# A SwiGLU layer by seven-product blocks: gate and up one product at a time in doubled banks, and the down projection with other signs, bank order and visits

## The chip, the core and the metric

The kernel is one inference step of a decoder layer and runs on one NeuronCore of a Trainium2 chip. It drives TensorE (PE, matrix products; PEld is its weight load), VectorE (DVE), ScalarE (ACT), GpSimd (POOL) and SyncE (SP, which here issues most DMAs). [...] The metric is the device time of one execution in microseconds (us), as the median of several runs.

## What is computed

The layer is attention and a gated delta rule on one projection, cross attention, and then SwiGLU. Only the last part changes:

```python
# x: 512 prompt rows and 32 sample rows of 2048 features; hidden width 5632
h = rmsnorm(x) * norm_ffn_g
gate, up = split(h @ w_gate_up)      # 2048 -> 2 x 5632
y = x + (silu(gate) * up) @ w_down   # 5632 -> 2048
```

All of it is held to float32 accuracy. A float32 matrix is therefore split into a high part (rounded to the float32r form that PE multiplies) and a low part (the rest), and a product is three: high by high, high by low, low by high.

## The kernel before

All 544 rows (T) are the columns of the moving operand; HT = 272 is half of them. Gate/up and down are both computed in 2 by 2 blocks with seven products instead of eight (the Winograd form of Strassen's scheme): two blocks of weight rows by two blocks of weight columns against two feature blocks by the two halves of T. The weight side needs four sums of weight blocks, the moving side four sums of feature blocks, and each result is a combination of the seven products. A matmul is 128 by 128 by 272.

**Gate/up** (lines 1740 to 1763 and the loop in `go`). There are 44 output blocks of 128 gate and 128 up columns. A block is four steps, a step takes two pairs of feature blocks and issues 7 products × 2 pairs × 3 terms = 42 matmuls (L1678). A step's products go to four accumulators: P16 (products 1 and 6, two banks), P7 (one), P45 (two), P23 (two), seven banks in all, held once. In the first three steps all high terms come first and then the low terms; in the last the terms go product by product. After the last step `combine` reads the banks (L1706 on ACT, L1707 to L1713 on DVE), then DVE scales by the row norm (L1731, L1732), ACT applies silu (L1726) and DVE multiplies (L1735).

**Weights of a step** (`Left`): SP loads two 256 KB pieces (raw, L1627) four steps ahead; POOL makes two sums of 256 columns (L1635, L1636) and DVE the two that depend on them (L1640, L1641); ACT rounds 768 raw and 1024 summed columns to high parts (wh, L1646); DVE subtracts them for the low parts (wl, L1653).

**Hidden values.** For each pair of finished blocks POOL makes the four moving-side sums (L1573 to L1576), ACT rounds (L1858), POOL makes low parts (L1859), and SP stores seven tiles to DRAM (hT, L1861).

**Down.** Sixteen output columns of 128, in eight blocks of two, against eleven groups of hidden pairs. Only a few groups fit in SBUF, so a block is visited several times (VISITS): each visit accumulates one or two groups, one step of 42 matmuls each. At the end of a visit the banks are taken to SBUF: first and seeded ones by an ACT copy (L1772), P16 and P7 by a DVE addition (L1770). At the start of a later visit P45 and P23 are seeded from SBUF by an ACT copy (L1759), in the last visit all four banks. POOL issues the loads of a group's 14 tiles (pr, L1835). After its second visit a block gets the residual x: SP loads two tiles (xl, L1780) into two slots, and POOL adds them (L1784 to L1786). The last visits are of groups 9 and 10 for all eight blocks, sixteen steps in a row; then the results are combined, transposed through PE (L961), scaled by ACT (L1968) and stored.

**What sets the order.** The FFN is written in a fixed order by `go`: for each step each engine's instructions stand in the order in which the code emits them, and no scheduler moves them. Each engine works through its own queue in that order, so an instruction that waits holds up what stands behind it on the same engine, DMA issues of SP and POOL among them.

## Time and profile before

| what | us |
|---|---|
| median of 3 runs | 3054.19 (3053.77 to 3056.27) |
| the profiled execution, its own time | 3052.51 |
| its span, first to last instruction | 3050.7 |
| first to last matmul of gate/up and down (L1678) | 1510.0 to 3037.1 |
| PE / DVE / ACT / POOL busy in the span | 2890.4 / 2265.9 / 1455.2 / 1149.7 |

The profile is of one execution. A group of instructions is named by its line, engine and operation, and by the tiles that it writes and reads (out<-in); behind the bar stand its busy time, the mean length of one in ns, and the idle time of its engine just before it with what ended that idle time. Matmuls are pipelined: each row lasts 0.29 us, but the next starts sooner, so PE can be busy all the time at different speeds. DMA issues are counted as they are issued; when a transfer lands is a separate entry.

### The profile page before, as it was taken

The numbers are of one execution on the slowest core, as the hardware profiler recorded it, in microseconds if no ns is written. First come the engines' busy times: TensorE is split into PE (matmuls) and PEld (weight loads), VectorE is DVE, ScalarE is ACT, GpSimd is POOL, SyncE is SP. The second block draws the span as 40 slices with busy tenths as digits, with TensorE's granted clock in tenths as the row PEclk, the third lists the DMA queues.
The fourth block names the chain that finished last, engine by engine and source line by source line (L and its number), as shares of the span: only waits on it lengthen the run. The fifth ranks groups of instructions, "written<-read, shape, count | busy, mean of one in ns | idle before, by whom it ended". The sixth has DMA issues, their size and how long they took to land. (4 is left out here: it accounts for less than half of the span.)

```text
span 3050.7 us, 58945 instructions
## 1 busy us (share of the span) xinstructions
PE 2890.4 (95%) x22118; PEld 2773.2 (91%) x22118; DVE 2265.9 (74%) x3513; ACT 1455.2 (48%) x2760; POOL 1149.7 (38%) x1444
## 2 busy tenths in 40 slices
...
GB/s 213 96 80 84 75 89 96 147 134 147 173 105 152 222 205 149 125 86 113 180 88 138 149 138 133 143 148 137 139 141 146 134 222 216 218 190 174 173 143 73
DMA packets 638647, 435.62 MB, mean 143 GB/s; under 512 B 38715, under 2 KB 568968, under 8 KB 638360
## 3 DMA queue, kind: packets, MB, share of 16 engines
...
## 5 line engine op out<-in xcount | busy, mean ns | idle before, releaser
L1678 PE MATMUL bank<-pr,wh 128*128 128x272 f32 x7392 | 1149.7, 291 | 70.1 <-ACT bank L1759 31.1
L1678 PEld LDWEIGHTS bank<-pr,wh 128*128 128x128 f32 x7392 | 1031.2, 190 | 89.9 <-ACT bank L1759 40.6
L1678 PE MATMUL bank<-pr,wl 128*128 128x272 f32 x3696 | 703.9, 289 | 1.2 <-DVE wl L1653 1.2
L1678 PEld LDWEIGHTS bank<-pr,wl 128*128 128x128 f32 x3696 | 556.9, 188 | 5.6 <-DVE wl L1653 5.6
L209 PE MATMUL mm<-ah,wh 128*128 128x272 f32 (+1 forms) x2464 | 538.1, 298 | 4.6 <-ACT ah L322 3.5
L209 PE MATMUL mm<-al,wh 128*128 128x272 f32 (+1 forms) x2464 | 524.2, 291 | 0.7 <-DVE al L240 0.7
L209 PE MATMUL mm<-ah,wl 128*128 128x272 f32 (+1 forms) x2464 | 515.6, 290 | 0.1
L1653 DVE TENSOR_TENSOR wl<-sum,wh 128x1024 fp32r<-128x1024 f32 x264 | 431.2, 1633 | 31.4 <-ACT wh L1646 30.6
L1646 ACT CAST wh<-sum 128x1024 fp32r<-128x1024 f32 x264 | 277.0, 1049 | 326.6 <-DVE sum L1641 322.2
L1635 POOL TENSOR_TENSOR sum<-raw 128x256 f32<-128x256 f32 x264 | 219.3, 831 | 561.3 <-DVE wl L1653 549.8
L1646 ACT CAST wh<-raw 128x768 fp32r<-128x768 f32 x264 | 220.6, 836 | 414.8 <-PE bank L1678 309.1
L209 PEld LDWEIGHTS mm<-ah,wh 128*128 128x128 f32 (+1 forms) x2464 | 391.6, 188 | 27.6 <-issue 8.5
L198 DVE TENSOR_TENSOR wl<-wr,wh 128x512 fp32r<-128x512 f32 (+1 forms) x366 | 262.7, 721 | 192.9 <-ACT wh L197 183.6
L209 PEld LDWEIGHTS mm<-al,wh 128*128 128x128 f32 (+1 forms) x2464 | 389.5, 188 | 5.4 <-issue 2.0
L209 PEld LDWEIGHTS mm<-ah,wl 128*128 128x128 f32 (+1 forms) x2464 | 386.4, 188 | 2.5 <-DVE wl L198 0.5
L197 ACT CAST wh<-wr 128x512 fp32r<-128x512 f32 (+1 forms) x366 | 224.3, 615 | 328.6 <-PE mm L209 272.2
L1653 DVE TENSOR_TENSOR wl<-raw,wh 128x768 fp32r<-128x768 f32 x264 | 293.3, 1111 | 86.0 <-PE bank L1678 75.6
L1636 POOL TENSOR_TENSOR sum<-raw 128x256 f32<-128x256 f32 x264 | 249.4, 945 | 0.0
L1641 DVE TENSOR_TENSOR sum<-raw,sum 128x256 f32<-128x256 f32 x264 | 199.3, 755 | 9.0
L1640 DVE TENSOR_TENSOR sum<-sum,raw 128x256 f32<-128x256 f32 x264 | 163.2, 618 | 7.2 <-POOL sum L1635 7.2
L1859 POOL TENSOR_TENSOR hs<-x,hs 128x544 fp32r<-128x544 f32 x44 | 76.1, 1729 | 52.8 <-issue 42.3
L1859 POOL TENSOR_TENSOR hs<-u,hs 128x272 fp32r<-128x272 f32 (+1 forms) x44 | 79.1, 1797 | 43.9 <-ACT hs L1858 43.9
...
## 6 DMA issues: line engine op xcount, KB each, us to landing
...
hT<-hs SPq DMA_DIRECT2D x154, 272.0 KB
pr<-hT POOLq DMA_DIRECT2D x154, 272.0 KB, 3.7
page<-in_cache_sb_k SPq DMA_DIRECT2D x128, 128.0 KB
...
```

The lines of the kernel that those rows point to most:

```text
L197: nc.scalar.copy(hi[:, :m, :n], raw[:, k : k + m, :n])
L198: nc.vector.tensor_sub(lo[:, :m, :n], raw[:, k : k + m, :n], hi[:, :m, :n].bitcast(F32))
L209: c.nc.tensor.matmul(ps[:n, h, :HT], l[:, :n], r[:, h * HT : (h + 1) * HT], start=first and i == 0, stop=last and i == 2,)
L1635: g.tensor_sub(self.sum[:, 2], a[:, 0], a[:, 2])
L1636: g.tensor_add(self.sum[:, 0], a[:, 0], a[:, 1])
L1640: v.tensor_add(b[:, 1], b[:, 2], a[:, 1])
L1641: v.tensor_sub(b[:, 3], a[:, 3], b[:, 1])
L1646: self.c.nc.scalar.copy(hi, x())
L1653: self.c.nc.vector.tensor_sub(lo, x, hi[:, :, :].bitcast(F32))
L1678: self.c.nc.tensor.matmul(self.c.bank[bank][:, o], self.left.part(low, li, i), r, start=new and not (i or low or n), stop=self.last and i ...
L1859: self.later(0, "pool", lambda: c.nc.gpsimd.tensor_sub(lo[:, o : o + n * HT], x[i][:, : n * HT], hi[:, : n * HT].bitcast(F32)))
```

## The change

**Gate/up.** A block is no longer four steps of two pairs but seven products, one after the other, in the order 1, 5, 6, 2, 7, 3, 4, each over all eight pairs: 24 matmuls into one bank. There are banks A, B and C, two sets used by blocks in turn, and one bank E for both. The combination happens in the banks: after product 1, ACT copies A to B (so that product 2 is added to it), after product 6 A to C (product 3 is added), and product 5 goes from E to SBUF (e). DVE then needs one operation on 272 columns for each quarter, and the row norm is applied to gate only where it is read; up's factor is left out there and made good where y is stored (`unscale`; and the residual x is multiplied by q, the inverse of both norms' factors).

Weights of a block are four loads of 512 KB (L1702), four sums of 1024 columns, all on DVE (L1708), seven high parts on ACT (L1715) and seven low parts on DVE (L1719), made two products ahead. All weight tiles share 13 slots of 4 KB. Of the eight pairs of x the last two are made while the first products run (ticks −1, 0, 2 and 3, a tick being one product), and four extra matmuls (`open`) touch the banks that ACT writes first.

**Down.** All three remaining sums are on DVE (L1757 to L1759: 512, 256 and 256 columns). The signs of the moving-side sums change with them. Visits that are not a block's last use the order 4, 5, 2, 3, 1, 6, 7, last visits 1, 6, 7, 4, 5, 2, 3. The visits are cut in another way: each block's first visit is of one group (for the second half of the blocks the second visit too), and at the end stand four blocks with groups 9 and 10 and four with 10 alone, twelve steps. The first two groups' operands are fetched from four and six ticks before the end of gate/up. The residual needs one tile slot for q, so x comes through one slot; POOL multiplies (L1851) and adds (L1853, L1854, L1856).

**The order.** `Work.at(tick, place, do)` notes what is emitted at which place of a tick; in gate/up a tick is a product, in down a step.

The diff, cut to its core:

```diff
-VISITS = ((0, (0,)), (1, (0, 1)), (0, (1, 2)), (1, (2, 3)), (0, (3, 4)), (1, (4, 5)), (0, (5, 6)), (1, (6, 7)), (0, (7, 8)), (1, (8,)),
-          (0, (9, 10)), (1, (9, 10)))
+VISITS = ((0, (0,)), (1, (0,)), (1, (1,)), (0, (1, 2)), (1, (2, 3)), (0, (3, 4)), (1, (4, 5)), (0, (5, 6)), (1, (6, 7)), (0, (7, 8)), (1, (8, 9)))
+LAST = (9, 10), (10,)
...
+W_TILES = 13
...
+    def at(self, tick, place, do):
+        self.n += 1
+        self.todo.setdefault(tick, []).append((place, self.n, do))
...
+GU_ORDER = (1, 5, 6, 2, 7, 3, 4)
...
+        for x, tick in (("21", -8), ("11", -8), ("22", -7), ("12", -3)):
+            at(self.t0 + tick, 5, lambda x=x: self.load(x))
+        for q, tick in ((7, -4), (5, -3), (6, -2), (3, 1)):
+            at(self.t0 + tick, 50, lambda q=q: self.sum(q))
+        for i, q in enumerate(GU_ORDER):
+            at(self.t0 + i - 2, 20, lambda q=q: self.high(q))
+            at(self.t0 + i - 2, 60, lambda q=q: self.low(q))
+            at(self.t0 + i, 30, lambda q=q: self.matmuls(q))
+        A, B, C, E = f.gu_banks[j % 2]
+        s, v = f.c.nc.scalar, f.c.nc.vector
+        g, u = [], []
+        rr = f.t_rr if j == 0 else 0
+        def left():
+            g.append(f.c.tt("g"))
+            v.tensor_mul(g[0][:, :HT], B, f.rr[:, :HT])
+        def lower():
+            u.append(f.c.tt("u"))
+            v.tensor_add(u[0][:, HT:], A, self.e)
+        def right():
+            v.tensor_add(g[0][:, HT:], C, self.e)
+            v.tensor_mul(g[0][:, HT:], g[0][:, HT:], f.rr[:, HT:])
+        def gate():
+            v.tensor_mul(u[0][:, :HT], A, g[0][:, :HT])
+            v.tensor_mul(u[0][:, HT:], u[0][:, HT:], g[0][:, HT:])
+            f.hidden(j, u[0])
+        def keep():
+            self.e = f.c.tt("e")[:, :HT]
+            s.copy(self.e, E)
+        at(self.t0 + 1, 10, lambda: s.copy(B, A))
+        at(self.t0 + 2, 10, keep)
+        at(self.t0 + 3, 10, lambda: s.copy(C, A))
+        at(max(rr, self.t0 + 4), 40, left)
+        at(self.t0 + 5, 40, lower)
+        at(max(rr, self.t0 + 6), 41, right)
+        at(max(rr, self.t0 + 6), 65, lambda: s.activation(g[0], g[0], AF.Silu))
+        at(max(rr, self.t0 + 6) + 1, 16 if j == NH - 1 else 42, gate)
...
+    def sum(self, q):
+        x, y = {5: ("21", "22"), 7: ("21", "11"), 6: ("22", 7), 3: ("12", 6)}[q]
+        self.a[q] = self.f.tile(F32, "sum")
+        self.f.c.nc.vector.tensor_sub(self.a[q], self.a[x], self.a[y])
...
+        bank = {5: E, 2: B, 3: C}.get(q, A)
+        terms = [(self.hi[q], i, r) for i in range(8) for r in range(2)] + [(self.lo[q], i, 0) for i in range(8)]
+        for n, (w, i, r) in enumerate(terms):
+            self.f.c.nc.tensor.matmul(
+                bank, w[:, i * P : (i + 1) * P], self.f.pairs[i].op[q][r], start=q in (1, 5) and n == 0, stop=n == 23, skip_group_check=True,
...
+    def sums(self):
+        a, v = self.raw, self.c.nc.vector
+        self.sum = b = self.f.tile(F32, "sum").rearrange("p (s m) -> p s m", s=4)
+        v.tensor_sub(b.rearrange("p (x s) m -> p x s m", s=2)[:, :, 0], bc(a[:, 0:1], [P, 2, 2 * P]), a[:, 1:3])
+        v.tensor_sub(b[:, 1], a[:, 1], b[:, 2])
+        v.tensor_sub(b[:, 3], a[:, 3], b[:, 1])
...
-        self.last = self.visit == 5
-        self.seeds = (P16, P7, P45, P23) if self.last else (P45, P23)
+        self.order = (1, 6, 7, 4, 5, 2, 3) if self.visit == self.end else (4, 5, 2, 3, 1, 6, 7)
+        self.seeds = () if not self.visit else (P45, P23, P16, P7) if self.visit == self.end else (P45, P23)
...
+        if bank in (P16, P7) and not new:
+            self.c.nc.vector.tensor_add(x, x, self.c.bank[bank])
+        else:
+            self.c.nc.scalar.copy(x, self.c.bank[bank])
...
-        y, z = (self.c.cst.tile([P, T], F32, tag="rstd", name="xl", bufs=2) for _ in range(2))
-        for i, x in enumerate((y, z)):
-            self.f.later(1, "sp", lambda i=i, x=x: self.c.nc.sync.dma_start(x, self.c.xT[self.m + i]))
-        def add():
-            g = self.c.nc.gpsimd
-            g.tensor_add(self.z, self.z, z)
-            g.tensor_add(self.y, self.y, y)
-            g.tensor_sub(self.y[:, HT:], self.y[:, HT:], z[:, HT:])
-        self.f.later(2, "pool", add)
...
+    def residual(self, tick):
+        c, at = self.c, self.f.work.at
+        xs = {}
+        def load(i):
+            xs[i] = c.cst.tile([P, T], F32, tag="rstd", name="xl", bufs=2)
+            c.nc.sync.dma_start(xs[i], c.xT[self.m + i])
+        def add(i):
+            g, x = c.nc.gpsimd, halves(xs[i])
+            y, z = self.parts[P23], self.parts[P45]
+            g.tensor_mul(x, x, halves(self.f.q))
+            if i:
+                g.tensor_add(z, z, x)
+                g.tensor_sub(y[:, 1], y[:, 1], x[:, 1])
+            else:
+                g.tensor_add(y, y, x)
+        for n, i in enumerate((1, 0)):
+            at(tick + 1 + n, 3, lambda i=i: load(i))
+            at(tick + 2 + n, 2, lambda i=i: add(i))
...
+        tiles = [(pair, n, k) for n in (3, 1, 2, 0) for pair in range(2) for k in range(2 if n else 1)]
+        for g in range(11):
+            a, b = used[g - 3][1] + 1 if g > 2 else (0, 1, 5)[g], used[g][0] - 1
+            for i, x in enumerate(tiles):
+                tick = t0 + a + i * min(b - a, 7) // 14 if g else t0 - (6 if i < 6 else 4)
+                at(tick, 90, lambda g=g, i=i, x=x: self.fetch(g, i, *x))
...
+        early = lambda n: tick - n if p >= n else self.t_down - 2 * (n - p)
+        at(early(4) if p >= 4 else self.t_down - 12 + 2 * p, 95, s.load)
+        at(early(2), 45, s.sums)
+        for i in range(2):
+            at(early(1), 20 + i, lambda i=i: s.high(i))
+            at(early(1), 50 + i, lambda i=i: s.low(i))
+        if p == 0:
+            at(tick, 28, lambda: (self.c.open_banks(), b.next_visit()))
+        for i in range(7):
+            at(tick, 30 + i, lambda i=i: s.matmuls(b.order[i]))
+        if not s.last:
+            return
+        def seed(*banks):
+            for x in banks:
+                if nb:
+                    nb.before(x)
+        if nb:
+            at(tick, 46, nb.next_visit)
+        if s.visit == b.end:
+            at(tick, 47, lambda: (b.combine(0), seed(P16, P7)))
+            at(tick, 60, lambda: (b.combine(1), seed(P45)))
+            at(tick, 61, lambda: (b.combine(2), seed(P23), self.out(tick, b)))
+        else:
+            at(tick, 60, lambda: (b.take(P45), seed(P45), b.take(P23), seed(P23)))
+            at(tick, 61, lambda: (b.take(P16), b.take(P7), seed(P16, P7)))
+        if s.visit == 1 + (b.m >= 8):
+            b.residual(tick)
```

Where the order moves, first in gate/up. PE, one whole step of a block before (bank_18768 is P16, 18769 P7, 18770 P45, 18771 P23):

```order
L1678 MATMUL bank_18768<-pr,wh 128x272 x8
L1678 MATMUL bank_18769<-pr,wh 128x272 x4
L1678 MATMUL bank_18770<-pr,wh 128x272 x8
L1678 MATMUL bank_18771<-pr,wh 128x272 x8
L1678 MATMUL bank_18768<-pr,wl 128x272 x4
L1678 MATMUL bank_18769<-pr,wl 128x272 x2
L1678 MATMUL bank_18770<-pr,wl 128x272 x4
L1678 MATMUL bank_18771<-pr,wl 128x272 x4
```

PE, most of one block now (gu_18776 is A of the second set, 18773 E, 18774 B, 18775 C):

```order
L1726 MATMUL gu_18776<-pr,wh 128x272 x16
L1726 MATMUL gu_18776<-pr,wl 128x272 x8
L1726 MATMUL gu_18773<-pr,wh 128x272 x16
L1726 MATMUL gu_18773<-pr,wl 128x272 x8
L1726 MATMUL gu_18776<-pr,wh 128x272 x16
L1726 MATMUL gu_18776<-pr,wl 128x272 x8
L1726 MATMUL gu_18774<-pr,wh 128x272 x16
L1726 MATMUL gu_18774<-pr,wl 128x272 x8
L1726 MATMUL gu_18776<-pr,wh 128x272 x16
L1726 MATMUL gu_18776<-pr,wl 128x272 x8
L1726 MATMUL gu_18775<-pr,wh 128x272 x16
L1726 MATMUL gu_18775<-pr,wl 128x272 x8
```

The step of 42 matmuls over all four accumulators, which came four times in a block, has become runs of 24 matmuls into one bank. A bank that was written in every step and read at the block's end is now written in one run or two and read between them.

DVE in the same stage, from the end of a block before (wl and sum are a step's weights; a, b, e, g, u the combination):

```order
L1707 TENSOR_TENSOR e_21688<-b_21687,bank0_18768 128x272
L1708 TENSOR_TENSOR e_21688<-e_21688,bank1_18769 128x272
L1640 TENSOR_TENSOR sum_21579<-sum_21579,raw_21511 128x256
L1641 TENSOR_TENSOR sum_21579<-raw_21511,sum_21579 128x256
L1710 TENSOR_TENSOR b_21687<-e_21688,bank2_18770 128x272
L1711 TENSOR_TENSOR u_21686<-e_21688,bank2_18770 128x544
L1713 TENSOR_TENSOR g_21685<-b_21687,bank3_18771 128x544
L1653 TENSOR_TENSOR wl_21706<-raw_21511,wh_21694 128x768
L1653 TENSOR_TENSOR wl_21708<-sum_21579,wh_21698 128x1024
L1640 TENSOR_TENSOR sum_21640<-sum_21640,raw_21576 128x256
L1641 TENSOR_TENSOR sum_21640<-raw_21576,sum_21640 128x256
L1731 TENSOR_TENSOR g_21685<-g_21685,rstd2_18964 128x544
```

DVE now, at the end of a block and the start of the next:

```order
L1719 TENSOR_TENSOR wl_22155<-raw_21928,wh_22125 128x1024
L1677 TENSOR_TENSOR g_22119<-gu5_18775,e_22030 128x272
L1678 TENSOR_TENSOR g_22119<-g_22119,rstd2_19001 128x272
L1719 TENSOR_TENSOR wl_22189<-sum_22121,wh_22161 128x1024
L1681 TENSOR_TENSOR u_22151<-gu6_18776,g_22119 128x272
L1682 TENSOR_TENSOR u_22151<-u_22151,g_22119 128x272
L1719 TENSOR_TENSOR wl_22222<-sum_22153,wh_22194 128x1024
L1708 TENSOR_TENSOR sum_22251<-raw_22091,sum_22153 128x1024
L1719 TENSOR_TENSOR wl_22253<-raw_22091,wh_22225 128x1024
L1719 TENSOR_TENSOR wl_22293<-sum_22087,wh_22267 128x1024
L1708 TENSOR_TENSOR sum_22322<-raw_22157,raw_22159 128x1024
L1719 TENSOR_TENSOR wl_22324<-sum_22251,wh_22296 128x1024
```

The combination of five operations in a row (L1707 to L1713) is gone from DVE's queue, and single operations of 272 columns stand between sums and low parts of 1024.

In the down projection, PE at the end of a visit and the start of the next, before:

```order
L1678 MATMUL bank_18771<-pr,wh 128x272 x2
L1678 MATMUL bank_18771<-pr,wl 128x272
L1678 MATMUL bank_18768<-pr,wh 128x272 x8
L1678 MATMUL bank_18769<-pr,wh 128x272 x4
L1678 MATMUL bank_18770<-pr,wh 128x272 x8
L1678 MATMUL bank_18771<-pr,wh 128x272 x8
L1678 MATMUL bank_18768<-pr,wl 128x272 x4
```

The same now (bank1 is P7, bank2 P45; wh and wl change where the next visit begins):

```order
L1780 MATMUL bank1_29403<-pr_29836,wl_30324 128x272
L1780 MATMUL bank1_29403<-pr_29911,wh_30274 128x272
L1780 MATMUL bank1_29403<-pr_29913,wh_30274 128x272
L1780 MATMUL bank1_29403<-pr_29911,wl_30324 128x272
L1780 MATMUL bank2_29404<-pr_29537,wh_30333 128x272
L1780 MATMUL bank2_29404<-pr_29539,wh_30333 128x272
L1780 MATMUL bank2_29404<-pr_29537,wl_30383 128x272
L1780 MATMUL bank2_29404<-pr_29541,wh_30333 128x272
L1780 MATMUL bank2_29404<-pr_29613,wh_30333 128x272
```

P23, the last bank of a visit, was followed by P16, P7 and, after twelve matmuls, P45; now P7 is last and P45 first.

SP around the residual before (xl are tiles of x, raw the weights of later steps):

```order
L1627 DMA raw_31230<-in_w_down 128x4x128 x2
L1780 DMA xl_31293<-xT_95 128x544
L1780 DMA xl_31294<-xT_95 128x544
L1627 DMA raw_31302<-in_w_down 128x4x128 x2
L1627 DMA raw_31367<-in_w_down 128x4x128 x2
L1780 DMA xl_31430<-xT_95 128x544
```

SP now:

```order
L1747 DMA raw_30397<-in_w_down 128x4x128 x2
L1846 DMA xl_30400<-xT_98 128x544
L1747 DMA raw_30460<-in_w_down 128x4x128 x2
L1846 DMA xl_30466<-xT_98 128x544
L1747 DMA raw_30528<-in_w_down 128x4x128 x2
L1846 DMA xl_30533<-xT_98 128x544
L1747 DMA raw_30589<-in_w_down 128x4x128 x2
L1846 DMA xl_30595<-xT_98 128x544
```

Two loads of x stood side by side in front of every second step's weights; now one stands in front of each step's weights, and each waits for POOL's last use of the tile before it.

## The prediction

> **What bounds the kernel now.** I read the engines' shares of the page first, then the busy time by stage, then the groups of each stage with the releaser of their idle time.

> ```profile
> span 3050.7 us, 58945 instructions
> PE 2890.4 (95%) x22118; PEld 2773.2 (91%) x22118; DVE 2265.9 (74%) x3513; ACT 1455.2 (48%) x2760; POOL 1149.7 (38%) x1444
> ```

> TensorE (PE) is busy 95% of the span. Its time can shrink only where it idles, since the change keeps 7392 + 3696 products (it adds four).

> ```profile
> core 0: us, PE busy (x) PEld busy (x) DVE busy (x) ACT busy (x) POOL busy (x), PEclk, DMA share, GB/s
> 1510.00:1551.00 41.00, 27.52 (x180) 25.95 (x181) 34.91 (x60) 25.23 (x46) 18.64 (x17) 0.78 0.29 93
> 1551.00:2499.00 948.00, 921.76 (x7225) 908.68 (x7224) 933.30 (x1029) 401.27 (x515) 564.67 (x523) 1.00 0.45 141
> 2499.00:2516.00 17.00, 9.19 (x47) 8.12 (x46) 7.24 (x12) 3.19 (x6) 11.38 (x21) 0.70 1.21 366
> 2516.00:2920.00 404.00, 379.83 (x2973) 373.53 (x2972) 296.12 (x347) 215.15 (x302) 232.38 (x299) 1.00 0.69 197
> 2920.00:3037.00 117.00, 101.38 (x741) 96.46 (x741) 67.38 (x103) 59.80 (x119) 21.63 (x28) 0.96 0.30 86
> 3037.00:3051.00 14.00, 4.17 (x24) 2.38 (x22) 3.43 (x7) 4.84 (x17) 0.00 (x0) 0.73 0.27 80
> 1538.00:1542.00 4.00, 3.72 (x20) 3.32 (x19) 3.33 (x8) 2.17 (x4) 0.00 (x0) 0.56 0.00 0
> 1560.00:1581.00 21.00, 21.00 (x170) 21.00 (x169) 18.47 (x25) 8.34 (x11) 6.57 (x9) 1.00 0.34 101
> ```

> Columns: window and length, busy time and rows that touch the window for each engine, granted clock, DMA share, GB/s. The row 1560 to 1581 is the inside of one gate/up block: 170 matmuls touch 21.00 us, and each lasts 0.288 us, so (21.00 + 0.288) / 170 = **0.1252 us** from one to the next. A block of 168 is worth 21.04 us, a down step of 42 is worth 5.26. Against that:
> - 1551 to 2499, 43 gate/up blocks: 43 × 21.04 = 905, it took 948. Lost: 43.
> - 2499 to 2516, the change to down: 47 × 0.1252 = 5.9 of 17. Lost: 11.
> - 2516 to 2920, most visits: 2973 × 0.1252 = 372 of 404. Lost: 32.
> - 2920 to 3037, last visits: 741 rows, 60 of them transposes, so 681 × 0.1252 = 85 of 117. Lost: 32, part of it the transposes.

> In gate/up DVE is busy 933.30 of 948 (98%): 21.7 us in a block of 22.05. There it is the engine that sets the pace, and PE's idle time shows it:

> ```profile
> L1678 PE MATMUL bank<-pr,wh 128*128 128x272 f32 x4817 | 711.9, 289 | 25.0 <-DVE u L1711 25.0
> L1653 DVE TENSOR_TENSOR wl<-sum,wh 128x1024 fp32r<-128x1024 f32 x172 | 306.7, 1783 | 0.3 <-ACT wh L1646 0.3
> L1636 POOL TENSOR_TENSOR sum<-raw 128x256 f32<-128x256 f32 x171 | 164.6, 963 | 0.0
> L1635 POOL TENSOR_TENSOR sum<-raw 128x256 f32<-128x256 f32 x171 | 142.8, 835 | 288.7 <-DVE wl L1653 288.7
> L1859 POOL TENSOR_TENSOR hs<-u,hs 128x272 fp32r<-128x272 f32 (+1 forms) x42 | 76.8, 1827 | 43.9 <-ACT hs L1858 43.9
> L1859 POOL TENSOR_TENSOR hs<-x,hs 128x544 fp32r<-128x544 f32 x42 | 73.2, 1744 | 51.1 <-issue 42.3 <-DMA raw<-in_w_gate_up 8.7
> ```

> PE waits 25.0 us for one thing, the combination L1711 that frees the single-buffered banks. The long DVE operation, wl of 1024 columns, took 1783 ns on average, and it is not always so long:

> ```profile
> L1653 DVE TENSOR_TENSOR wl<-sum,wh x172: 1209/1759/3064, 1552.5 to 2496.5; 128x1024 fp32r<-128x1024 f32 x172
> ```

> ```profile
> 2658.10 1.22 DVE L1653 TENSOR_TENSOR wl<-sum,wh 128x1024 fp32r<-128x1024 f32 x1
> 2659.40 0.85 POOL L1635 TENSOR_TENSOR sum<-raw 128x256 f32<-128x256 f32 x1 [2.14 <-DVE wl L1653]
> ...
> 2662.42 2.08 POOL L1785 TENSOR_TENSOR a<-a,xl 128x544 f32<-128x544 f32 x1
> ...
> 2663.20 2.38 DVE L1653 TENSOR_TENSOR wl<-sum,wh 128x1024 fp32r<-128x1024 f32 x1
> ```

> Beside a quiet POOL it takes 1.22, beside POOL's L1785 2.38. So a part of DVE's load is POOL's doing.

> **The change, part by part.** Times are set against the profiled execution, 3052.51 us (span 3050.7, so 1.8 around it); it lies 1.7 under the median 3054.19.

> *Gate/up.* The bank waits go: products accumulate one after another in banks doubled by block, and every read of a bank lies at least one product (24 × 0.1252 = 3.0 us) before the next write to it. The question is whether DVE now keeps up. Small operations for scale:

> ```profile
> L1708 DVE TENSOR_TENSOR e<-e,bank x44: 437/438/440, 1548.2 to 2498.2; 128x272 f32<-128x272 f32 x44
> L1711 DVE TENSOR_TENSOR u<-e,bank x44: 705/712/717, 1550.1 to 2500.1; 128x544 f32<-128x544 f32 x44
> ```

> New DVE load of a block: seven wl and four sums, all 1024 wide, and six of 272 columns at 0.44: 11 × 1.21 + 6 × 0.44 = 15.9 us beside a quiet POOL. Old load, by width between these prices (four steps with wl of 1024 at 1.21, of 768 at 0.95 and two sums at 0.42; then three operations of 272 at 0.44 and five of 544 at 0.71): 16.9, measured 21.7; so 4.8 us of stretch beside 564.67 / 43 = 13.1 us of POOL, 0.37 us each. POOL loses its weight sums, 164.6 + 142.8 = 307 us of 565, and keeps some 6 us a block, mostly L1859 and the sums for down. New DVE load: 15.9 + 0.37 × 6 = 18.1 of 21.04. That leaves 14%, and weights are made two products ahead, which covers single busy products. PE becomes the bound: the 43 us shrink to about 2, **−41**. Bounds: nothing gained if the 1024-wide operations stay at 1783 ns (11 × 1.783 + 2.6 = 22.2, the old pace), −43 at best. ACT is busy 401 of 948 and has three copies more a block, but smaller combination work; no bound. The four added matmuls cost 4 × 0.1252 = 0.5.

> *First block.* It needs eight pairs' first parts before it can go on, where the old one needed two; but then it no longer waits in the middle. 1510 to 1551 holds 168 × 0.1252 = 21 us of products in 41. The producers of x are the same, so I take **−2** (0 to −6).

> *Change to down.* The first operands are now fetched four to six products (12 to 18 us) before the first step; a fetch takes 3.7 (below). The 11 lost fall to 1: **−10** (0 to −11, as the stores of the last gate block may still be late).

> *Visits.* Groups of 2516 to 2920:

> ```profile
> L1678 PE MATMUL bank<-pr,wh 128*128 128x272 f32 x1982 | 329.4, 289 | 24.2 <-ACT bank L1759 23.7 <-ACT a L1772 0.5
> ...
> L1646 ACT CAST wh<-sum 128x1024 fp32r<-128x1024 f32 x71 | 74.2, 1046 | 5.1 <-DVE sum L1641 5.1
> ...
> L1646 ACT CAST wh<-raw 128x768 fp32r<-128x768 f32 x70 | 58.5, 836 | 177.1 <-PE bank L1678 168.8 <-issue 7.4 <-ACT hs L1858 0.9
> ...
> L1772 ACT COPY a<-bank 128x544 f32<-128x544 f32 x92 | 53.7, 590 | 3.9 <-PE bank L1678 3.5
> ...
> L1759 ACT COPY bank<-a 128x544 f32<-128x544 f32 x64 | 39.5, 617 | 2.0
> ```

> PE idles 24.2 us, 23.7 of it for the seed copy L1759. Before, the seeded banks P45 and P23 were the last to finish in a visit and came after only twelve matmuls (1.5 us) of the next; taking (0.59) and seeding (0.62) two banks does not fit there. Now they finish first, 24 of 42 matmuls in, so 2.25 us remain in the step for 2 × (0.59 + 0.62) = 2.4, and the P23 seed is wanted only 1.5 us into the next. P16 and P7, last in a visit, are needed last in the next. ACT's own load in a one-step visit is 0.84 + 1.05 + 2.4 = 4.3 of 5.26, so it fits. DVE takes over POOL's two sums as one of 512 columns (0.68 by width): 3.7 us a step with its wl and other sums, 4.8 where it also takes P16 and P7. **−30** (−20 to −32).

> *Last visits.* Sixteen steps become twelve plus four elsewhere, and the order 1, 6, 7, 4, 5, 2, 3 lets combination and seeding of the first banks run under the later products:

> ```profile
> L1678 PE MATMUL bank<-pr,wh 128*128 128x272 f32 x454 | 80.9, 306 | 7.4 <-ACT bank L1759 7.4
> ...
> L1968 ACT ACTIVATE y<-aux,unscale 128x128 f32<-128x128 f32 x48 | 13.6, 365 | 36.2 <-PE aux L961 36.2
> ...
> L961 PE MATMUL aux<-ident,a 128*128 128x128 f32 x48 | 7.4, 276 | 8.2 <-ACT y L1968 8.2
> ```

> 7.4 us of waiting for L1759 go, 8.2 for y shrink as the output transposes are spread over places in a step. In three steps (15.8 us) ACT has 3 × 1.89 of casts, 2 × 2.5 of seeds and 16 × 0.28 of y (13.6 / 48): 15.1, nearly all. So I keep 15 of 32: **−17** (−8 to −22).

> *Residual, the part that costs.* x is now loaded into one slot (the other holds the factor q), so each of a block's two loads waits for POOL's last use of the one before, and these loads stand in SP's queue ahead of the weight loads L1747. Behind them wait the raw weights, then DVE's sums, then PE. The nearest rows:

> ```profile
> L1784 POOL TENSOR_TENSOR a<-a,xl x8: 1352/1360/1376, 2591.3 to 2672.7; 128x544 f32<-128x544 f32 x8
> L1785 POOL TENSOR_TENSOR a<-a,xl x8: 2059/2074/2092, 2592.6 to 2674.0; 128x544 f32<-128x544 f32 x8
> L1786 POOL TENSOR_TENSOR a<-a,xl x8: 1636/1641/1651, 2594.8 to 2676.2; 128x272 f32<-128x272 f32 x8
> ```

> ```profile
> pr<-hT POOLq DMA_DIRECT2D x154, 272.0 KB, 3.7
> ```

> ```profile
> SPq L1780 <- POOL a L1786: 6.4, 5, 1.3
> ```

> A load of the same size lands in 3.7. A block needs two landings, four 544-wide operations (1.36 quiet, 2.07 beside DVE) and one of 272 (at most 1.64; half of 1.36 quiet, 0.7): between 7.4 + 5.4 + 0.7 = 13.5 and 7.4 + 8.3 + 1.6 = 17.3. PE gives it two steps, 10.5. Over eight blocks the chain falls behind by 24 to 54; four steps of loads ahead, of which sums take two, absorb about 9 (10.5 less a landing, plus the time from sum to product). So PE loses 15 to 45; with DVE busy 73% here I take 15.0 a block: 8 × 4.5 − 9 = **+27**. The old chain with two slots made SP wait 6.4 in all. If weights already in flight cover more than I think, this is 0 to 10.

> *DMA.* At 2499 the share was 1.21 with 366 GB/s, so some 300 GB/s fill the engines. Three groups are now fetched in the first steps beside weights: **+3** (0 to +10).

> *Tail.*

> ```profile
> L1706 ACT COPY a<-bank x8: 387/402/403, 2929.7 to 3038.9; 128x272 f32<-128x272 f32 x8
> L1713 DVE TENSOR_TENSOR a<-a,bank x8: 720/721/722, 2933.4 to 3041.4; 128x544 f32<-128x544 f32 x8
> ```

> The last combination started at 3038.9 after the last matmul; its first two stages now lie under the last two products: **−3** (0 to −5).

> Sum: −41 − 2 − 10 − 30 − 17 + 27 + 3 − 3 = −73, so 3052.5 − 73 = 2979.5 for an execution like the profiled, and 1.7 more against the median: **2981 us**.

> **The clock.**

> ```profile
> PE bank L1678 <- ACT bank L1759: 23.7, 28, 0.9
> ```

> After the 16 us gap in the first block the granted clock in 1538 to 1542 was 0.56, and 20 matmuls touched 4 us, 0.21 us each. If the residual's waits come bundled in one per block, each costs such a slow stretch too: 8 × 1.7 = 14 us (3.4 us at half rate). [...]

> **Rivals.**
> 1. *The residual is hidden* (weights in flight cover it): 2981 − 27 = 2954. For it: POOL is idle 43% of this stage and the chain may run at its quiet price. Against: 13.5 still exceeds 10.5. Chance 0.15.
> 2. *It is worse than I think*: 17.3 a block and the slow clock, +18 + 14: 3013. Chance 0.13.
> 3. *The change doesn't do what it says in gate/up*: DVE remains the pace at 22 us a block because its operations stay as long as before: 2981 + 41 = 3022. For it: eleven wide operations, more SBUF traffic than before. Against: POOL's half is gone. Chance 0.12.
> 4. *Slower*: the same mechanism, but worse. Sums on DVE are now in line with wl, so every stretch counts eleven times. To lose all 73, a block has to take 73 / 43 = 1.7 us more than 21.0, so a mean of (22.7 − 2.6) / 11 = 1.83 us for a 1024-wide operation; from there it is slower. At 2.38, the price beside a busy POOL, a block takes 28.8, and the time is 2981 + 43 × 7.8 = 3316. Half way, at 2.0, 3140. For it: 1.78 is the mean measured now. Against: it was measured beside twice the POOL work. Chance 0.08, with 0.03 for landing within 0.2%.

> **How the numbers follow.** Forecast 0.49, rivals 0.15, 0.13, 0.12, 0.08, no difference 0.03. Faster by over 0.2% (some 6 us, about what a measurement of this kernel can tell): 0.49 + 0.15 + 0.13 + 0.12 = 0.89; same 0.03; slower 0.08. The forecast's own terms spread some ±20. The range that leaves out rival 4, the no-difference case and the ends of the others is 2940 to 3028.

> **What would show it.** Gate/up right: 43 blocks in 905 to 910 us, DVE busy 83 to 90% there, mean of wl near 1.4. Wrong (rivals 3, 4): DVE 98% again and PE idle until DVE wl. Visits right: no idle until the seed copies in the down stage before the last visits. Residual right: a stretch of some 110 us from the fourteenth down step in which PE idles until DVE wl or sums, SP waits for POOL at the x loads, clock near 1.00. Transition right: no PE idle until the fetch at the first step. Most likely to be wrong is the residual's +27, then the first block.

## The result and the profile after

| | before | after |
|---|---|---|
| median, us (runs, lowest to highest) | 3054.81 (4, 3053.77 to 3056.27) | **3002.99** (4, 2998.29 to 3007.62) |
| ratio, 95% interval | | 0.983 (0.9813 to 0.9847) |
| the profiled execution, us | 3052.51 | 3001.82 |

The kernel is 1.7% faster, and the interval lies clear of 1. The time lies 22 us above the prediction and inside its range. First the engines' shares on the page of after:

```profile
span 3000.1 us, 56822 instructions
PE 2881.7 (96%) x22122; PEld 2772.6 (92%) x22122; DVE 2096.9 (70%) x3302; ACT 1490.5 (50%) x2820; POOL 731.8 (24%) x932
```

Then the busy time of each engine by stage, the stages cut where the prediction's terms begin and end (the last three columns are granted clock, DMA share, GB/s):

```profile
1510.00:1552.00 42.00, 28.33 (x171) 25.58 (x170) 34.99 (x50) 25.20 (x44) 7.94 (x8) 0.77 0.38 116
1552.00:2460.00 908.00, 906.14 (x7233) 905.23 (x7231) 731.15 (x743) 422.28 (x560) 288.37 (x183) 1.00 0.50 149
2460.00:2502.00 42.00, 41.60 (x333) 41.61 (x334) 33.21 (x42) 32.04 (x53) 18.46 (x27) 1.00 0.78 228
2502.00:2533.00 31.00, 25.76 (x182) 24.28 (x180) 17.01 (x27) 19.62 (x28) 11.70 (x23) 0.94 1.09 321
2533.00:2553.00 20.00, 19.88 (x159) 19.82 (x159) 18.66 (x25) 10.22 (x14) 5.52 (x3) 1.00 0.46 134
2553.00:2661.00 108.00, 97.50 (x719) 91.14 (x719) 103.36 (x103) 51.56 (x68) 66.15 (x65) 1.00 0.67 192
2661.00:2886.00 225.00, 223.80 (x1774) 222.06 (x1773) 174.82 (x258) 126.68 (x169) 37.10 (x70) 1.00 0.65 188
2886.00:2987.00 101.00, 86.99 (x603) 82.06 (x602) 59.88 (x97) 54.07 (x116) 0.00 (x0) 0.92 0.29 83
2987.00:3000.00 13.00, 3.91 (x18) 2.13 (x16) 3.43 (x7) 3.68 (x13) 0.00 (x0) 0.61 0.24 69
```

Four of these rows have no hole: gate/up after its first block, the change to down (2460 to 2502, 41.60 of 42), and the visits in 2533 to 2553 and 2661 to 2886. Beside the first block and the tail, three have one: 2502 to 2533, 2553 to 2661, and the last visits, where the granted clock is 0.92 as well.

Taken matmul by matmul, from the start of each block or step to the next, and with 5.26 us for a down step of 42:

| stage, us | before | after | e12 | e13 |
|---|---|---|---|---|
| first gate/up block | 40.7 | 42.4 | 42.6 | 42.6 |
| the other 43 blocks | 948.2 | 908.1 | 908.1 | 908.1 |
| down step 0 | 16.7 | 5.4 | 5.4 | 5.4 |
| lost in steps 9 to 12 | 1.1 | 8.8 | 8.8 | 2.8 |
| lost in steps 16 to 41 | 14.4 | 20.0 | 19.5 | 15.3 |
| lost in the other steps | 16.4 | 2.0 | 2.4 | 1.1 |
| lost in the last visits (16 steps before, 12 since) | 32.0 | 33.3 | 19.2 | 18.7 |
| last matmul to end of span | 13.6 | 12.7 | 10.4 | 10.2 |

The differences of the first two columns sum to −50.4 of the 50.7 us between the two profiled executions. (e12 and e13 are experiments below.)

**Gate/up.** The two wide forms of DVE's low parts in 1552 to 2460, and PE's matmuls, in the view of groups:

```profile
L1726 PE MATMUL gu<-pr,wh 128*128 128x272 f32 x4816 | 652.1, 288 | 0.1
L1726 PE MATMUL gu<-pr,wl 128*128 128x272 f32 x2412 | 351.5, 288 | 1.3 <-DVE wl L1719 1.3
L1719 DVE TENSOR_TENSOR wl<-sum,wh 128x1024 fp32r<-128x1024 f32 x172 | 211.0, 1227 | 83.5 <-ACT wh L1715 83.1 <-issue 0.2
L1719 DVE TENSOR_TENSOR wl<-raw,wh 128x1024 fp32r<-128x1024 f32 x128 | 196.4, 1534 | 5.2 <-ACT hs L1932 0.5 <-PE gu L1726 0.4
```

PE's idle time there fell from 25.0 to 1.4 us. The mean of wl is (211.0 + 196.4) / 300 = 1.36 us (1.78 before for the form of 1024 columns made from sums), DVE is busy 731.15 / 43 = 17.0 us a block, 81%.

**Residual.** The loads of x and POOL's work on them, from the view of the tile xl, and what SP's queue waited for in 2550 to 2661 (total, times, longest):

```profile
L1846 SPq DMA_DIRECT2D xl<-xT x16: 338/339/504, 2541.1 to 2642.7; - x16
L1851 POOL TENSOR_TENSOR xl<-xl,rstd x16: 1353/1362/2106, 2544.9 to 2646.0; 128x544 f32<-128x544 f32 x16
L1853 POOL TENSOR_TENSOR a<-a,xl x8: 1414/1426/2233, 2547.1 to 2640.4; 128x544 f32<-128x544 f32 x8
L1854 POOL TENSOR_TENSOR a<-a,xl x8: 947/957/1477, 2549.3 to 2641.8; 128x272 f32<-128x272 f32 x8
```

```profile
SPq L1846 <- POOL a L1854: 32.1, 8, 4.4
SPq L1846 <- POOL a L1856: 22.7, 7, 3.4
SPq L1747 <- DVE wl L1770: 15.8, 15, 5.6
```

Sixteen loads stand 101.6 / 15 = 6.77 us apart, 13.5 a block, and each is issued when POOL has done with the tile of the one before: SP waits 32.1 + 22.7 us for POOL there. This is the chain that the prediction named, and with one load in front of each step's weights it is slower than PE's 5.26 us. In the third row, weight loads wait for wl to free one of the 13 shared slots. From a weight load's issue to its first matmul the trace has 18.1 us on average in steps 17 to 32 (21.1 before); but in steps 42 to 70, where almost nothing is lost, it is 17.8 as well, so this lead alone does not explain the loss.

DVE is a second limit in the same place. Steps 16 to 41 of after:

```profile
2553.30:2710.10 156.80, 145.57 (x1095) 138.33 (x1094) 141.53 (x157) 79.80 (x106) 73.57 (x79) 1.00 0.66 191
```

DVE is busy 141.53 / 26 = 5.44 us a step, more than the 5.26 that PE needs. From 2710 to 2866, with POOL busy 29.68 us, the same work took it 119.40 us in 29.6 steps, 4.0 each. PE's only row of waits in steps 16 to 41, 9.4 us, is for wl, which DVE makes.

**The step that fell furthest from its number: the last visits.** The waits of 2890 to 2988:

```profile
ACT bank L1802 <- DVE a L1835: 18.2, 7, 2.6
DVE a L1831 <- ACT a L1830: 13.8, 4, 4.3
...
DVE ys L2043 <- PE aux L2041: 13.3, 5, 4.7
PE bank L1780 <- ACT bank L1802: 12.0, 7, 2.5
...
ACT bank L1802 <- DVE a L1831: 11.1, 7, 3.6
```

PE waits for the seed copy L1802 at six of the seven boundaries between last visits (the seventh wait is the one before them); the new bank order took this wait out of the other visits. L1802 waits for the first operations of the combination, ACT's copy L1830 and then DVE's L1831. The timeline shows why they are late, in two ways that take turns. At the ends of three blocks with two steps it is DVE (rows with what ended the idle time before them in brackets):

```profile
2923.91 0.47 DVE L2043 TENSOR_SCALAR ys<-aux,unscale 32x256 f32<-32x256 f32 x1 [4.74 <-issue]
...
2924.31 0.67 DVE L1757 TENSOR_TENSOR sum<-raw 128x512 f32<-128x512 f32 x1
...
2925.81 0.43 DVE L1831 TENSOR_TENSOR a<-a,bank 128x272 f32<-128x272 f32 x1
2926.28 0.93 ACT L1802 COPY bank<-a 128x544 f32<-128x544 f32 x2 [3.59 <-DVE a L1831]
...
2926.95 0.51 PE L1780 MATMUL bank<-pr,wh 128*128 128x272 f32 x2 [2.48 <-ACT bank L1802]
```

DVE stands 4.74 us in front of ys, the store of the block before, whose transposes are placed late in the step. Behind it in DVE's queue come three weight sums (none at the last of the three) and only then L1831, which reads P16. P16 had been finished some 6 us before, twelve matmuls after the step's start at 2918.36; the order of DVE's queue, not the bank, made it late. At the ends of three blocks with one step it is ACT:

```profile
2934.92 1.14 ACT L2036 ACTIVATE y<-aux,unscale 128x128 f32<-128x128 f32 x4 [0.99 <-PE aux L964]
...
2935.94 0.40 ACT L1830 COPY a<-bank 128x272 f32<-128x272 f32 x1
...
2936.37 0.44 DVE L1831 TENSOR_TENSOR a<-a,bank 128x272 f32<-128x272 f32 x1 [4.33 <-ACT a L1830]
```

Here DVE stands idle for 4.33 us, and the copy L1830, the first operation of the combination, stands in ACT's queue behind eight y operations of the block before, the last four of which waited for their transposes. The two kinds cost PE about the same: 2.48 + 2.38 + 0.86 = 5.7 us of idle time behind DVE, 3 × 1.87 = 5.6 behind ACT. After the first of these gaps, 1.87 us long, the granted clock went from 1.00 to 0.50 for 3.41 us:

```profile
2908.07:2911.48 3.41, 1.27 (x8) 0.86 (x7) 2.36 (x4) 1.85 (x6) 0.00 (x0) 1.00 0.70 193
2911.48:2914.90 3.42, 3.42 (x17) 3.11 (x15) 2.22 (x4) 1.68 (x3) 0.00 (x0) 0.50 0.31 90
2911.50:2914.30 2.80, 2.80 (x14) 2.63 (x12) 2.20 (x4) 1.08 (x2) 0.00 (x0) 0.50 0.34 103
```

Some 1.4 us after PE starts again at 2910.13, 14 matmuls take 2.80 us at a granted clock of 0.50: 2.80 − 14 × 0.1252 = 1.0 us more than at full rate.

### The profile page after: what moved, and what is told of

It reads as the page before. It is cut to its first block, busy times and chain, and to the rows that moved or that the text cites. A ratio compares the mean times of both kernels' runs of the same rounds, so it can differ in the third digit from the quotient of the medians.

```text
span 3000.1 us, 56822 instructions
## 1 busy us (share of the span) xinstructions
PE 2881.7 (96%) x22122; PEld 2772.6 (92%) x22122; DVE 2096.9 (70%) x3302; ACT 1490.5 (50%) x2820; POOL 731.8 (24%) x932
## 4 chain that ended last, share of the span: by engine, by line
PE 54%; DVE 5%; DMA 2%; issue 1%; ACT 1%; SPq 0%; DVEq 0%; ACTq 0%
PE gu L1726 30%; PE bank L1780 11%; PE mm L212 8%; DVE wl L1770 2%; PE aux L1346 2%; PE mm L1534 2%; DMA raw<-in_w_down 1%; PE aux L964 1%; DVE sum L1758 1%; PE aux L754 0%; DVE sum L1757 0%; DVE sum L1759 0%; DMA raw<-in_w_gate_up 0%; DVE a L1820 0%; PE aux L1420 0%
## 5 line engine op out<-in xcount | busy, mean ns | idle before, releaser
L1726 PE MATMUL gu<-pr,wh 128*128 128x272 f32 x4928 | 673.1, 289 | 13.1 <-ACT pr L1601 12.1
L1726 PEld LDWEIGHTS gu<-pr,wh 128*128 128x128 f32 x4928 | 639.6, 189 | 15.7 <-ACT pr L1601 13.3
L1780 PE MATMUL bank<-pr,wh 128*128 128x272 f32 x2464 | 474.6, 291 | 12.6 <-ACT bank L1802 12.0
L212 PEld LDWEIGHTS mm<-ah,wh 128*128 128x128 f32 (+1 forms) x2464 | 391.1, 188 | 28.8 <-issue 8.5
L1780 PEld LDWEIGHTS bank<-pr,wh 128*128 128x128 f32 x2464 | 391.5, 191 | 14.6 <-ACT bank L1802 13.6
L1780 PE MATMUL bank<-pr,wl 128*128 128x272 f32 x1232 | 364.2, 296 | 18.7 <-DVE wl L1770 15.8
L1726 PE MATMUL gu<-pr,wl 128*128 128x272 f32 x2464 | 359.8, 288 | 1.3 <-DVE wl L1719 1.3
L1726 PEld LDWEIGHTS gu<-pr,wl 128*128 128x128 f32 x2464 | 328.9, 189 | 1.6 <-DVE wl L1719 1.6
L1719 DVE TENSOR_TENSOR wl<-sum,wh 128x1024 fp32r<-128x1024 f32 x176 | 215.9, 1226 | 83.5 <-ACT wh L1715 83.1
L1715 ACT CAST wh<-sum 128x1024 fp32r<-128x1024 f32 x176 | 185.0, 1051 | 164.2 <-DVE wl L1719 156.1
L1780 PEld LDWEIGHTS bank<-pr,wl 128*128 128x128 f32 x1232 | 235.2, 191 | 30.8 <-DVE wl L1770 30.6
L1719 DVE TENSOR_TENSOR wl<-raw,wh 128x1024 fp32r<-128x1024 f32 x132 | 201.3, 1525 | 5.2 <-ACT hs L1932 0.5
L1715 ACT CAST wh<-raw 128x1024 fp32r<-128x1024 f32 x132 | 138.9, 1053 | 95.7 <-DVE sum L1708 72.9
L1708 DVE TENSOR_TENSOR sum<-raw,sum 128x1024 f32<-128x1024 f32 x88 | 125.4, 1425 | 29.6 <-PE gu L1726 29.6
## 6 DMA issues: line engine op xcount, KB each, us to landing
hT<-hs SPq DMA_DIRECT2D x154, 272.0 KB
pr<-hT POOLq DMA_DIRECT2D x154, 272.0 KB, 7.0
```

The costliest lines, as they stand in the source:

```text
L212: c.nc.tensor.matmul(ps[:n, h, :HT], l[:, :n], r[:, h * HT : (h + 1) * HT], start=first and i == 0, stop=last and i == 2,)
L1708: self.f.c.nc.vector.tensor_sub(self.a[q], self.a[x], self.a[y])
L1715: self.f.c.nc.scalar.copy(self.hi[q], self.left(q))
L1719: self.f.c.nc.vector.tensor_sub(self.lo[q], self.left(q), self.hi[q].bitcast(F32))
L1726: self.f.c.nc.tensor.matmul(bank, w[:, i * P : (i + 1) * P], self.f.pairs[i].op[q][r], start=q in (1, 5) and n == 0, stop=n == 23, skip_gr ...
L1780: self.c.nc.tensor.matmul(self.c.bank[bank][:, o], t[x][:, s, i * P : (i + 1) * P], pairs[i].op[q][r], start=new and not (i or n), stop=se ...
```

## The experiments

Runs on different chips are compared by the ratio of their times to those of the kernel before on the same chip. "Lost" is read from the trace as in the table above.

**e4, is it the second set of banks?** Both sets use one A.

```diff
-        at(max(rr, self.t0 + 6) + 1, 16 if j == NH - 1 else 42, gate)
+        at(max(rr, self.t0 + 6) + 1, 16 if j == NH - 1 else 29, gate)
-        self.gu_banks = (A0, B0, C0, E), (A1, B1, C1, E)
+        self.gu_banks = (A0, B0, C0, E), (A0, B1, C1, E)
```

> The changed kernel, but both sets of gate/up banks use the same bank A, and the gate multiplication that reads A stands ahead of the next block's first product. Theory (the doubled banks are what removed the wait of 1 us a block): PE waits for gate at the start of every block, about 0.7 to 1.2 us after the last product (scale, silu and multiplication stand before it), 43 blocks lose 30 to 50 us together, gate/up takes 980 to 1000 us and the time is about 3033 to 3053. Rival (relief of DVE was what counted, the bank wait only its shadow): blocks stay at 21.0 to 21.3 us, the time within 10 us of 3003.

Measured 3044.7 (one run). The values of the first gate block change, since its gate reads A after the next block's first product. The 43 blocks take 952.8 us, 44.7 more than after: 1.04 a block. PE's groups in e4:

```profile
L1726 PE MATMUL gu<-pr,wh 128*128 128x272 f32 x4592 | 628.0, 289 | 32.1 <-DVE u L1681 32.1
```

With one A, PE waits for the operation that reads it, as it waited for L1711 before, although DVE is no busier (631.68 us of 850 from 1600 to 2450, 686.59 in after). So without the doubled bank the whole gain of this stage is gone, however much room DVE has. Whether the second A would be enough beside the old DVE load, 98% busy and 21.7 us a block, no run shows.

**e5, is it POOL's relief?** Two of the four weight sums go to POOL.

```diff
-        self.f.c.nc.vector.tensor_sub(self.a[q], self.a[x], self.a[y])
+        (self.f.c.nc.gpsimd if q in (5, 7) else self.f.c.nc.vector).tensor_sub(self.a[q], self.a[x], self.a[y])
```

> The changed kernel, but two of the four weight sums of a gate/up block (5 and 7) are made by POOL again. Theory (PE is the bound of gate/up and DVE has room): POOL's busy time in gate/up rises from 288 to over 550 us, DVE's wl operations get longer beside it, DVE's busy time there stays between 700 and 850 of 907 us, and blocks stay at 21.0 to 21.2 us: time within 8 us of 3003. Rival (it is the move of the sums off POOL that bought gate/up its time): blocks go back towards 22 us, 30 us or more slower.

Measured 3006.0 (one run, inside the spread of after's four), 908.9 us for the 43 blocks. The window 1600 to 2450 of after, then of e5:

```profile
1600.00:2450.00 850.00, 848.60 (x6777) 848.16 (x6775) 686.59 (x693) 398.06 (x530) 274.24 (x172) 1.00 0.50 148
```

```profile
1600.00:2450.00 850.00, 848.23 (x6770) 847.35 (x6769) 673.01 (x611) 395.11 (x525) 496.67 (x242) 1.00 0.50 148
```

DVE has 82 operations fewer, at 1.22 us quiet some 100 us, but its busy time falls by 13.6 only: beside 222.4 us more of POOL the others stretched by 86, 0.39 us for each us of POOL. The prediction had 0.37. But the 43 blocks took only 0.8 us more for it (908.9 against 908.1), with DVE busy 673.01 of 850 us. That POOL became quiet was not needed for the gain.

**e8, is it the bank order of the visits?** The old order of the banks in all visits.

```diff
-        self.order = (1, 6, 7, 4, 5, 2, 3) if self.visit == self.end else (4, 5, 2, 3, 1, 6, 7)
+        self.order = (1, 6, 7, 4, 5, 2, 3) if self.visit == self.end else (1, 6, 7, 4, 5, 2, 3)
```

> The changed kernel, but the visits that are not a block's last use the order 1, 6, 7, 4, 5, 2, 3 again, so that P23 and P45 are last in a visit and P45 is needed again after 18 matmuls. Theory (the order of the banks is what removed 1.1 us at the start of each visit): the first step of each later visit is 0.8 to 1.5 us longer, 28 visits, the time is 20 to 35 us longer, about 3025 to 3037. Rival (the doubled slots and the earlier casts did it): within 6 us of 3003.

Measured 3024.88 (one run): down takes 550.7 us instead of 527.0. The other steps lose 27.1 instead of 2.0; steps 16 to 41 lose 21.3, only 1.3 more, probably since PE is already waiting there. PE's waits from 2460 to 2900:

```profile
PE bank L1780 <- DVE a L1820: 24.8, 13, 3.4
PE bank L1780 <- ACT a L1822: 11.1, 9, 1.9
```

The takes are back in PE's way. The order does what the prediction's −30 says.

**e1, e6 and e10, the residual.** e1 issues the loads of x from POOL, so that weights no longer stand behind them; e6 spreads the residuals of the eight blocks over more steps; e10 does both.

```diff
# e1, e10
-            c.nc.sync.dma_start(xs[i], c.xT[self.m + i])
+            c.nc.gpsimd.dma_start(xs[i], c.xT[self.m + i])
# e6, e10
-            b.residual(tick)
+            b.residual(tick + b.m // 2)
```

> The changed kernel, but POOL issues the loads of x for the residual itself, so SP's weight loads no longer stand behind a load that waits for POOL. Theory (the residual's waits cost PE because weight loads queue behind them on SP): the down steps 16 to 33, which take 6.3 to 6.9 us each in the changed kernel, fall to about 5.3 to 5.5, the waits of SP for POOL at the x loads (55 us in that stretch) go, and the time falls by 15 to 20 us, to about 2985. Rival (the chain of load, multiply and add on POOL costs PE in any case, through operands fetched late by POOL or parts that are wanted for the next seed): the steps stay above 6 us and the time within 5 us of 3003.

> The changed kernel, but the residual of the blocks is spread: one block in three steps instead of one in two, with the same operations, the same slot and the same queues. Theory (in those steps the work does not fit: the chain of load and POOL operations takes 13.5 us for two steps of 10.5, and beside POOL DVE is busy 106 of 111 us): with 15.8 us for a block both fit, steps 16 to 38 fall to 5.3 to 5.5, and the time falls by 15 to 20 us to about 2985. Rival (any wait of SP at an x load delays the weights behind it, so the cost goes by the number of loads): the 16 loads still cost PE 0.5 to 1 us each and the time falls by less than 8.

> The changed kernel with both residual edits: x is loaded from POOL's queue and the blocks are spread, one in three steps. Apart they brought 5 and 7 us. Theory (two costs: weight loads queued behind x loads on SP, with only 2 to 4 us between landing and use of the weights, and DVE stretched beside POOL): both gone, steps 16 to 41 lose under 6 us instead of 21, time about 2984 to 2990. Rival (weight loads land late in this stretch whatever stands ahead of them, since their slots come free late): single steps of 7 to 10 us remain, the loss stays over 12 us, time 2993 or more.

| | median (lowest to highest) | ratio (95%) | lost in steps 16 to 41, profiled execution |
|---|---|---|---|
| after | 3002.99 (2998.29 to 3007.62) | 0.983 (0.9813 to 0.9847) | 20.0 |
| e1 | 2997.91 (2996.54 to 3003.59) | 0.9817 (0.9799 to 0.9835) | 14.7 |
| e6 | 2995.81 (2992.81 to 3000.37) | 0.9808 (0.9792 to 0.9824) | 17.5 |
| e10 | 3000.23 (2994.53 to 3003.45) | 0.9821 (0.9805 to 0.9838) | 9.5 |

In the profiled executions e1 and e10 lose less in the stretch. For e6 this is less sure: seven kernels that leave the residual alone (e2 to e5, e7, e9, e12) lose 18.2 to 22.1. The times don't tell the four apart, since their intervals overlap, and none of the three brought the 13 to 20 us that its theory expected. In e1, SP's queue is free of x, and what remains of the loss includes one step that is 10.8 us long. Before it DVE waits 5.9 us for the weights' DMA: the fetches of a group, held behind x in POOL's queue until 2656, were then issued in a row, and the DMA share from 2656 to 2676 is 1.13 (0.71 in after). Elsewhere in e1's stretch DVE is nearly full, 106.33 of 108 us:

```profile
2547.00:2655.00 108.00, 102.81 (x798) 100.18 (x797) 106.33 (x114) 57.78 (x77) 74.76 (x70) 1.00 0.63 179
```

So in e10's profiled execution, the fastest of its four, 20.0 − 9.5 = 10.5 of this loss hang on where x is loaded and when. The chain's length alone is not the cause: e6 gives a block 15.8 us for its 13.5 and still loses 17.5. How much of the loss is DVE's own load is open. Two slots for x, the nearest test, were not tried.

**e3 and e9, the crowd of fetches.** Both spread the fetch of the third group's operands; e9 also moves the second's away from the first's.

```diff
# e3
-                tick = t0 + a + i * min(b - a, 7) // 14 if g else t0 - (6 if i < 6 else 4)
+                tick = t0 + a + i * min(b - a, 12 if g == 3 else 7) // 14 if g else t0 - (6 if i < 6 else 4)
# e9
-            a, b = used[g - 3][1] + 1 if g > 2 else (0, 1, 5)[g], used[g][0] - 1
+            a, b = used[g - 3][1] + 1 if g > 3 else (0, 1, 7, 12)[g], used[g][0] - 1
```

> The changed kernel, but the fetch of group 3 is spread over 12 steps instead of 7, so that fewer fetches of three groups lie on top of one another in steps 5 to 15. Theory (the 9 us lost in steps 9 to 12 are weight loads that land late beside the fetches): steps 9 to 12 lose 3 to 5 us instead of 9, the down stage gets 4 to 6 us shorter. Rival (the weight loads are late because their slots come free late, whatever the fetches do): steps 9 to 12 still lose 8 to 9.

> The changed kernel, but group 2 is fetched in steps 7 to 11 and group 3 in steps 12 to 19, instead of 5 to 11 and 8 to 14, so that never two groups are fetched at once after step 7. Spreading group 3 alone (the run before) left the loss of steps 9 to 12 as it was; the weights wanted there are issued in steps 5 to 9, where groups 1 and 2 overlap (about 100 GB/s of weights and 230 of fetches against some 300). Theory (fetches of two groups at once make the weight loads late): issue to use of the weights of steps 9 to 12 falls from 11.0 us to 8 or less, and these steps lose under 4 us instead of 9; down 4 to 7 us shorter. Rival (something else in that stretch, such as the last hidden stores): they lose 8 or more.

Measured 3002.33 and 3000.26 (one run each); steps 9 to 12 lose 9.5 and 6.4. The window 2496 to 2521 of after (e3 has a DMA share of 1.21 at 359 GB/s there, e9 1.19 at 358):

```profile
2496.00:2521.00 25.00, 22.59 (x164) 21.92 (x163) 14.10 (x21) 17.27 (x27) 14.12 (x27) 0.93 1.20 363
```

The DMA share is much the same in all three. The place in the program did not move the transfers: POOL had nothing in front of the fetches that would wait, so it issued them as soon as their tiles were free. So these two runs did not test the crowd; e13 does.

**e2, e7 and e12, the last visits.** e2 puts the first stage of the combination, ACT's copy with it, and its seeds further ahead in both queues: on DVE ahead of ys and the sums, on ACT ahead of the y operations of that step. e7 also puts the next step's low parts ahead of the combination. e12 also puts the seeds of P45 and P23, which the next visit needs late, behind ACT's casts.

```diff
# e2, e7, e12
-            at(tick, 46, nb.next_visit)
+            at(tick, 32.1 if s.visit == b.end else 46, nb.next_visit)
-            at(tick, 47, lambda: (b.combine(0), seed(P16, P7)))
+            at(tick, 32.2, lambda: (b.combine(0), seed(P16, P7)))
# e7, e12 (ends: the steps with a last visit)
-            at(early(1), 50 + i, lambda i=i: s.low(i))
+            at(early(1), (31.5 if p - 1 in self.ends else 50) + i / 10, lambda i=i: s.low(i))
# e12
-            at(tick, 60, lambda: (b.combine(1), seed(P45)))
-            at(tick, 61, lambda: (b.combine(2), seed(P23), self.out(tick, b)))
+            at(tick, 60, lambda: b.combine(1))
+            at(tick, 61, lambda: (b.combine(2), self.out(tick, b)))
+            at(tick + 1, 25, lambda: seed(P45, P23))
```

> The changed kernel, but in a block's last visit the first stage of the combination and the seeds of P16 and P7 stand in the queues directly behind product 7 of that step, ahead of the output's ys and of the weight sums on DVE. Theory (the last visits stayed at 8 to 10 us a step because combine and seeds stand behind other DVE work, and PE needs the P16 seed first in the next visit): PE's 12 to 14 us until the seed copy there shrink to under 4, the granted clock of that stretch rises from 0.91 to 0.95 or more, steps 78 to 87 fall from 86 us in sum to 70 to 75, the time by 11 to 16 us, to about 2990. Rival (ACT is nearly full there with y, casts and seeds, as the prediction reckoned): the steps keep 8 us or more and the time falls by less than 4.

> The changed kernel with the first stage of the last visits' combination ahead of ys and sums as in the run before (which still had one step in three of 11.7 us, in which ACT waited 5.6 us for the combination's second stage behind DVE's sums and low parts, with the next step's casts queued behind it), and in addition the next step's low parts ahead of it on DVE. Theory: the low parts are then in time, the long steps fall from 11.7 to 7 to 9, steps 78 to 87 from 77 to 64 to 70, time about 2980 to 2986. Rival (DVE itself is full in these steps: 3 x 3.7 of weights and 2 x 2.8 of combination and ys, 17.6 us in three steps of 15.8): three steps stay at 22 us or more and the time at 2989 to 2993.

> The changed kernel with the last visits' combination in two parts: first stage and low parts ahead as in the run before, and the seeds of P45 and P23 moved on ACT behind the next casts, so that ACT does not stand still for the combination's second stage. Theory (order on ACT, not its load, is what keeps one step in three at 11 us): PE's waits for y of 8.5 us and for wl shrink, steps 78 to 87 fall from 76 to 63 to 70 us, time about 2980 to 2986. Rival (DVE is full there): 74 us or more, time 2990 to 2994.

| | median (lowest to highest) | ratio (95%) | lost in the last visits |
|---|---|---|---|
| e2 | 2991.42 (2990.49 to 2992.93) | 0.9791 (0.9774 to 0.9807) | 24.7 |
| e7 | 2993.24 (2991.19 to 2994.81) | 0.9801 (0.9784 to 0.9817) | 23.9 |
| e12 | 2986.75 (2985.3 to 2992.33) | 0.9777 (0.9758 to 0.9796) | 19.2 |

e2 moves two lines of the order and recovers 8.6 of the 33.3; its interval lies below that of after. In it PE waits for L1802 only 0.7 us in all, but L1802 now waits longer, for L1835 of the second combination:

```profile
ACT bank L1802 <- DVE a L1835: 22.8, 7, 5.6
```

That wait holds up ACT's casts, which stand behind it. The low parts (e7) add nothing that can be told; taking the seeds out of the casts' way (e12) brings another 4.7 in the profiled executions (the intervals of e7 and e12 overlap). Steps 78 to 87 take 71.8 us in e12, between its two expectations. The stage in e2, then in e12:

```profile
2886.00:2977.00 91.00, 79.58 (x592) 76.14 (x591) 61.20 (x99) 53.61 (x116) 0.00 (x0) 0.96 0.31 92
```

```profile
2886.00:2973.00 87.00, 77.27 (x604) 74.34 (x604) 63.01 (x103) 54.69 (x116) 0.00 (x0) 1.00 0.35 100
```

The granted clock of this stage is 0.92 in after, 0.96 in e2 and 1.00 in e12: with the combination moved up PE's waits got shorter, and in e12 no slow stretch is left.

**e13, all of it, with POOL tied to PE's pace.** e12, e6 and e9 together, and in steps 7 to 19 a two-element addition on POOL that reads the step's low part, so that the fetches behind it wait for DVE. Its result is not used.

```diff
+        if 6 < p < 20:
+            at(tick, 89, lambda: self.c.nc.gpsimd.tensor_add(self.c.small([P, 2]), *[s.lo[1][:, 0, 0:2].bitcast(F32)] * 2))
```

> The order of the last visits as in the run before (E12), the residual spread as in E6, the fetches of groups 2 and 3 apart as in E9, and new: in steps 7 to 19 a two-element addition on POOL that reads the step's low weights stands ahead of the step's fetches, so that POOL cannot issue them ahead of PE. In the runs with spread fetches POOL issued 5 fetches in 5 us all the same, because nothing held its queue back, and the DMA share stayed at 1.20 with 360 GB/s from 2496 to 2521: those runs did not change what they were to change. Theory (fetches of two groups, issued as fast as POOL can, make the weights of steps 9 to 12 land 11 us after issue): with pacing the share in steps 7 to 12 falls under 1.0, issue to use of these weights to 8 us or less, steps 9 to 12 lose under 4 us instead of 8 to 9. Rival (the weights are late there for another reason): they lose 8 or more at a lower share. Whole kernel: by the theory 2976 to 2984, by the rival 2982 to 2988.

Measured **2972.61 (2968.95 to 2975.37, five runs)** against 3055.42 of the kernel before on that chip: 0.9724 (0.9711 to 0.9737), faster than both kernels. The crowd is gone:

```profile
2496.00:2521.00 25.00, 22.71 (x180) 22.27 (x179) 17.90 (x27) 19.30 (x30) 10.30 (x21) 1.00 1.01 294
```

DMA share 1.01 instead of 1.20, 180 matmul rows instead of 164, and steps 9 to 12 lose 2.8 instead of 8.8. From the issue of their weights to the first use of them, a sum on DVE, it takes 9.0 us there, 11.0 in after and 6.5 in after's steps 4 to 8. The share and the 9.0 us stayed above what was expected (under 1.0, 8 or less), but the loss fell as expected. So it was the crowd that made the weights late. Of the 12.5 us between the profiled executions of e12 and e13, 6.0 are in these steps and 4.2 in steps 16 to 41.

## Why the prediction was right, and where it was not

It was right in the bound, in the sign and in where most gains and losses lie; the sum came out at −50.7 instead of −73. Of the 22 us between them, 18 are the last visits.

- **43 blocks, −41: measured −40.1.** A block takes 21.12 us on average, 21.04 at full rate; DVE 17.0 us a block, 18.1 forecast. e4 shows that the doubled bank is needed for it. The prediction read DVE as the engine that set the old pace; e4 has that pace with a DVE that is only 74% busy (631.68 of 850 us from 1600 to 2450). The worry about DVE (rivals 3 and 4) had no ground: even e5, with POOL as busy as before, keeps the pace.
- **First block, −2: measured +1.7.** The wait in the middle is gone, as forecast: the kernel before waited 8.8 + 4.4 us for the row norm there (its L271 and L961). But the need for eight pairs at once, which the prediction named without a price, costs 12.1 us of waiting for ACT's pairs (L1601). No run tests it.
- **Change to down, −10: measured −11.3.** Step 0 takes 5.4 us.
- **Visits −30, residual +27, DMA +3: 0 in all, measured −1.1** (7.7 + 5.6 − 14.4). The three can be told apart only in part. Outside the two stretches the loss is 2.0, and e8 puts 25.1 of it back: the visits are right. That the three came out so near their sum is luck: the residual lost 7 less than its 27, the DMA 4.7 more than its 3.
- **Residual.** Its chain is in the trace, with a price of 13.5 a block, the lower end of the range given, and not 15.0, as POOL's operations ran at their quiet price (1.36 and 1.43 us) beside a DVE that was busy 96%. By the prediction's own sum eight blocks then fall behind by 8 × (13.5 − 10.5) = 24, and 15 are lost after the 9 that the weights in flight were to absorb; 20.0 were. Either the weights absorbed less, or something else cost time beside the chain. DVE did run short: the prediction put it at 3.7 to 4.8 us a step in the visits, without a stretch beside POOL, and it took 5.44 of 5.26. As e6 and e1 lose 17.5 and 14.7 with the chain relaxed or off SP's queue, the 20.0 can't be put down to the chain alone, and how it divides is open. The clock there stayed at 1.00, as forecast, so that rival 2 fell; rival 1 fell with the 20.0.
- **DMA, +3: measured +7.7,** inside its 0 to 10. e13 shows the crowd as its cause.
- **Last visits, −17: measured +1.3. This step failed.** The prediction said that the order "lets combination and seeding of the first banks run under the later products". The banks were finished in time, but `combine(0)` stands at place 47 of a step: its copy on ACT behind the y operations, its additions on DVE behind ys and the sums. The prediction counted ACT's load for these steps and did not read the order in either queue. PE still waited 12.0 us for the seed copies that were to run under the later products, where 7.4 were to go. With the combination moved up (e2) and the seeds behind the casts (e12) the stage loses 19.2, near the 15 that the prediction kept: what was forecast is there, but not in this order of DVE and ACT.
- **The clock.** The forecast has no term for it, and the 1.7 us of rival 2 for a slow stretch are an estimate from the first block of before, 20 × (0.21 − 0.1252); one in the last visits of after cost some 1 us. In the last visits a gap of 1.87 idle us (2.16 from one matmul's start to the next) was followed by half rate. The mean of 0.92 over 101 us makes 16 us at half rate, some 6 us of lost time in the 33.3. The last visits of before have three stretches of 3.41 us at 0.50 as well, from 2947.80, 2978.52 and 3009.24.
- **Tail, −3: measured −0.9.** Not followed up.
